# One hybrid mixer block with a conv-FFN on one core: where two of h's Strassen operands are split into high and low parts, when a gelu is issued, and the order of the last outputs

## The chip, the cores and the metric

The kernel runs on 1 core of one Trainium2 chip. The metric is the device time of one launch in microseconds (us). Engine names as the profile has them: PE (TensorE matmul), PEld (its weight loads), DVE (VectorE), ACT (ScalarE), POOL (GpSimd), SP (SyncE, here only a DMA queue). A second DMA queue is issued by POOL.

## The reference, cut to what matters

One transformer block on x of shape (1, 1024, 1024): token mixers, an output projection with residual and layer norm, and then the FFN, which is the part the change touches:

```python
def conv_ffn(h, w_up, conv_w, conv_b, w_down, grid_rows):
    a, g = jnp.split(h @ w_up, 2, axis=-1)                 # 1024 -> 2 x 2816
    a = dwconv3x3(a.reshape(...16 rows x 64 columns...), conv_w) + conv_b
    return (jax.nn.gelu(a, approximate=False) * g) @ w_down  # 2816 -> 1024

x_new = layer_norm(ALPHA * x_new + mx[5] * ffn_x, ln2_g[l], ln2_b[l])
```

Everything is float32. Products are made of two float32r parts of each operand, high and low: hi*hi + hi*lo + lo*hi, so three matmuls where one float32r matmul would be one.

## The kernel before

**Stages.** To about 690 us of the span: mixers, output projection, first layer norm and what prepares the FFN's first product. From there to about 1077 us `ffn_up`, then `ffn_down` to the end.

**ffn_up.** The 2816 hidden columns are 22 units f of 128 columns (hidden on partitions, 1024 tokens in the free dimension as two halves of 512). Each unit is made of seven block products in Winograd's form of Strassen's scheme; a product k is 12 matmuls of 128x128 by 128x512 (four pieces, three matmuls each). A unit's products run in the order 1, 2, 6, 5, 7, 3, 4 (`self.plan`, line 1111; units 1 and 2 are started by hand before the loop, lines 1213 to 1266, where the last two are product 4 of units 1 and 2; unit 0 is made without the scheme). Product 1, 6, 7, 4 add into one PSUM bank `u.x` (tag B), 2 into `u.zv[:, 0]`, 5 and 3 into `u.zv[:, 1]`, where `zv` is one of only two pairs of banks (tag A). `after(k)` (line 1333) is what follows a product:

- ACT copies banks out (`s`, `r`), DVE adds (`a`), ACT `centre` writes the middle tap of the 3x3 convolution into `zv`, DVE `conv` adds the other eight taps (8 instructions). So DVE does one unit's convolution while PE does the next unit's products.
- `b.prev.gelu()` comes after product 6 of the next unit (ACT reads the whole pair `zv`, which is then free), `finish` after its product 5 (DVE multiplies by the gate: `h` is ready, and its store to `hd[f]` is issued), `fetch` loads `hd[f - 11]` for the upper units.
- `b.made.sums()` (line 1410) comes after products 1 and 2 of the unit after that. For units 0 to 10 POOL makes h[:,0] - h[:,1] and SP stores it to `s3[f]`; for units 11 to 21 POOL makes two sums of h of units f and f - 11 and stores them to `s12[f - 11]`.

`prepare(n)` (line 1049) keeps the weights five products ahead: POOL makes the sums of raw weights (`combine`), ACT the high part (`wf[:, 0]`), and POOL the low part (`wf[:, 1]`, always one form later, `low`). All engines run their instructions in program order (`self.pinned`).

**From ffn_up to ffn_down.** In the last unit `down_first` (line 1287) makes the first three items of `ffn_down` ahead: high parts on ACT, low parts on POOL (tiles `dwh`, `dwl`, `dwv`). In `after(3)` of the last unit the sums of unit 20 stand ahead of its convolution (line 1364).

**ffn_down.** The same scheme over tokens, hidden and output columns: `plan` has 77 items (k, f), k in the order 1, 2, 6, 5, 3, 7, 4, f from 0 to 10; each item is 12 matmuls (4 blocks t of 128 tokens, three each). Products 1, 6, 7, 4 add into the banks `X[t]`, products 2, 5, 3 into `Y[t]`. For item i in iteration i: `load(i + 8)` (SP loads h's part and, where it is not on chip, w's part into a tile `raw`), `high(i + 5)` (ACT, two casts: h's half `[:, 0]` and w's half `[:, 1]` of the pair of tiles x = forms[i]), `low(i + 4)` (DVE, from item 5 on; two subtractions), then the matmuls. A pair of tiles is used again by item i + 8. For products 5, 7 (last 3 items) and 4 (last 5 items) the last items are held back and run together, block by block (`group`, line 1450): blocks 2 and 3 first, then 0, then 1.

**Outputs.** Tokens 0 to 511 (t 0 to 3) get their two column halves from X and Y during products 2 to 7, in pieces put into `todo`, of which one (two in the first five items of product 7) is issued at the end of an iteration. `out(t, c, bank, add)` (line 1561) returns the pieces: `begin` (DVE adds the bank to y), `mid` (POOL loads the residual x into a tile `fx`, DVE multiplies y by the gate), `end` (DVE: y = ALPHA x + y, then batch statistics). `chain` makes mean and 1/sigma of the rows (ACT does the square root), `last(t, c)` the layer norm's scale and shift, two DVE instructions on 512 columns, and the store. Tokens 512 to 1023 follow behind product 4: `out`, `chain`, `last` for blocks 2 and 3, then 0, then 1.

## Time and profile before

| | |
|---|---|
| time before, median of 3 runs | 1317.91 us (1316.45 to 1319.5) |
| the profiled execution's own time | 1315.14 us |
| its span, first to last instruction | 1313.4 us |
| PE busy | 1244.1 us, 95% |
| DVE busy | 1015.4 us, 77% |
| ACT busy | 550.9 us, 42% |
| POOL busy | 363.4 us, 28% |
| mean granted TensorE clock | 0.990 of full |
| HBM read, written | 168.32 MB, 39.08 MB |

"Busy" is the time in which an engine ran at least one instruction. PE at 95% does not say that it ran at its best rate; the granted clock tells which of two levels (1.2 and 2.4 GHz) it had. A share over the whole span says little for one stage, so the rows below are taken stage by stage. The time of a launch is a little longer than the span, since starting and ending stand around it.

### The profile page before, as it was taken

Reading aid. Unit: us, or ns where it says so; the run is one execution under the profiler, and the core shown is the slowest. Engines: PE = TensorE matmul, PEld = TensorE weight load, DVE = VectorE, ACT = ScalarE, POOL = GpSimd, SP = SyncE. Lnnn points to the kernel's source line nnn. Section 1 sums busy time; section 2 is a strip of 40 time slices with the busy share of each in tenths; the row PEclk is TensorE's granted clock in tenths of the full one; section 3 lists DMA queues with packets and bytes.
Section 4 is the critical chain, followed back from the end, with each engine's and each line's share of the span. In section 5 each row is a group of like instructions: output and inputs, shape, how many; then the busy total and the mean of one; then the engine's idle time right before and its main releaser. Section 6 shows DMA issues by size and latency. Waiting matters only on the chain. (4 is left out here: it accounts for less than half of the span.)

```text
span 1313.4 us, 17643 instructions
## 1 busy us (share of the span) xinstructions
PE 1244.1 (95%) x6348; PEld 1044.6 (80%) x6348; DVE 1015.4 (77%) x1790; ACT 550.9 (42%) x980; POOL 363.4 (28%) x309
## 2 busy tenths in 40 slices
PE   4999999999999989999998999999999999999993
PEld 3887888889888878777876788888888888888872
DVE  7968984686949768697797777777766776988797
ACT  4836444443332241345363444444344443545420
POOL 0000000000000000000017788888988872000020
PEclk9999999999999999999999999999999999999997
DMA  9763234104123054346564434542443268999242
GB/s 332 265 198 124 96 121 152 49 24 159 54 71 113 17 178 144 124 167 206 172 188 135 172 117 159 177 136 89 160 145 124 101 228 306 352 312 363 88 145 89
DMA packets 99672, 208.56 MB, mean 159 GB/s; under 512 B 10224, under 2 KB 31360, under 8 KB 99584
## 3 DMA queue, kind: packets, MB, share of 16 engines
q1 hardware_dynamic: 94784, 190.65, 42.7%
q0 software_dynamic: 4800, 16.78, 3.5%
q8 instruction: 50, 0.82, 0.2%
q14 instruction: 38, 0.31, 0.1%
HBM read 168.32 MB, written 39.08 MB: 158 GB/s over the span
## 5 line engine op out<-in xcount | busy, mean ns | idle before, releaser
L57 DVE SCALAR_TENSOR_TENSOR psA<-a,par,psA 128x945 f32<-128x945 f32 (+2 forms) x176 | 215.9, 1227 | 21.6 <-ACT psA L57 16.2
L57 PE MATMUL psA<-x,wf 128*128 128x512 f32 x708 | 172.2, 392 | 6.4 <-ACT h L57 3.4
L57 PE MATMUL psB<-xk,wf 128*128 128x512 f32 x672 | 176.7, 390 | 0.9 <-ACT s L57 0.9
L57 PEld LDWEIGHTS psA<-x,wf 128*128 128x128 f32 x708 | 133.8, 189 | 35.8 <-ACT psA L57 3.9
L57 PEld LDWEIGHTS psB<-xk,wf 128*128 128x128 f32 x672 | 126.1, 188 | 27.7 <-ACT s L57 1.3
L57 POOL DMA_DIRECT2D wd<-pk x16 | 8.7, 542 | 500.7 <-ACT pk L57 463.0
L57 PE MATMUL psA<-xh,wh 128*128 128x512 f32 x320 | 126.8, 396 | 2.0 <-ACT wh L57 1.2
L57 POOL TENSOR_TENSOR wf<-raw,wf 128x512 fp32r<-128x512 f32 x95 | 123.1, 1301 | 20.0 <-ACT wf L57 19.4
L57 PE MATMUL psA<-xh,wl 128*128 128x512 f32 x320 | 126.1, 394 | 0.1
L57 PE MATMUL psA<-xl,wh 128*128 128x512 f32 x320 | 125.9, 393 | 0.0
L57 PE MATMUL psB<-x,wf 128*128 128x512 f32 x384 | 104.7, 389 | 0.0
L57 PEld LDWEIGHTS psB<-x,wf 128*128 128x128 f32 x384 | 72.0, 188 | 15.3 <-issue 0.2
L57 ACT CAST wh<-r 128x512 fp32r<-128x512 f32 x76 | 44.5, 619 | 84.7 <-PE psA L57 57.3
L57 ACT CAST wf<-raw 128x512 fp32r<-128x512 f32 x95 | 58.7, 618 | 47.5 <-PE psA L57 27.4
L57 DVE TENSOR_TENSOR a<-psA,s 128x512 f32<-128x512 f32 x39 | 27.0, 691 | 60.6 <-PE psA L57 59.0
L57 PEld LDWEIGHTS psA<-xh,wh 128*128 128x128 f32 x320 | 60.2, 188 | 14.1 <-ACT wh L57 1.6
L57 PEld LDWEIGHTS psA<-xh,wl 128*128 128x128 f32 x320 | 60.2, 188 | 12.4 <-DVE wl L57 0.5
L57 PEld LDWEIGHTS psA<-xl,wh 128*128 128x128 f32 x320 | 60.2, 188 | 11.7 <-issue 0.2
L57 DVE TENSOR_TENSOR kq<-kq,F 128x1024 f32<-128x1024 f32 x56 | 67.5, 1216 | 0.2
L57 DVE TENSOR_TENSOR wl<-r,wh 128x512 fp32r<-128x512 f32 x76 | 49.9, 687 | 22.4 <-PE psB L57 13.2
L57 ACT CAST fh<-dr 128x512 fp32r<-128x512 f32 (+1 forms) x47 | 36.1, 768 | 72.8 <-DMA dr<-in_w_down 22.2
L57 PE MATMUL psB<-kq,A 128*128 128x128 f32 x448 | 60.4, 289 | 0.8 <-ACT A L57 0.7
(365 smaller groups left out, 2928.9 us busy)
## 6 DMA issues: line engine op xcount, KB each, us to landing
raw<-in_wup SPq DMA_DIRECT2D x38, 512.0 KB, 5.5
ada<-in_ada SPq DMA_DIRECT2D x32, 512.0 KB, 4.4
r<-in_win SPq DMA_DIRECT2D x56, 256.0 KB, 2.8
ex<-in_w_down SPq DMA_DIRECT2D x55, 256.0 KB, 5.4
dr<-hd SPq DMA_DIRECT2D x44, 256.0 KB, 5.4
hd<-h SPq DMA_DIRECT2D x20, 512.0 KB, 3.0
dr<-s SPq DMA_DIRECT2D x33, 256.0 KB, 5.3
adat<-in_ada SPq DMA_DIRECT2D x16, 512.0 KB, 7.0
```

The lines of the kernel that those rows point to most:

```text
L57: ins = f(*args, **kw)
```

## The change

Five edits.

1. `sums` now has three parts. For units 0 to 10 POOL's difference is written in place (into h[:,0]); for units 0 to 20 ACT also makes the high part of one operand (the difference for 0 to 10, h[:,1] for 11 to 20) into a new tile `hp`, POOL its low part, and both (512 KB) are stored: to `s3` for units 0 to 10, to the new `a22` for 11 to 20. They come after products 1, 2 and 6 of the unit after next.
2. In `ffn_down` the items of product 7 and those of product 4 but its last (`made(i)`, 21 items) no longer load h's part in `load(i)`. Instead `high(i)` issues two loads on SP of the ready high and low parts straight into the forms, and ACT and DVE each do one instruction of 512 columns (w's half) where they did two.
3. In the part by hand `u1.gelu()` moves from behind product 4 of unit 1 to ahead of `u2.centre(1)`, with one `prepare` ahead of it; the sums of units 0 and 1 move into unit 3.
4. The sums of unit 20 move from ahead of the last convolution to behind the last product of unit 21.
5. The second column half of tokens 0 to 511 is made in another order: `early` (gate and residual on what is in y) in product 3's first items, `late` (bank times gate into an `fx` tile) and `late2` (add, statistics) in product 7. `last` works on 1024 columns at once, but for the very last block (t = 1 of the second half), and product 7's `todo` shrinks from 17 pieces to 9.

```diff
-        u0.sums()[0]()
         u1.conv()
         go(u2, 3)
         tt(out=u2.a[:, 1], in0=u2.v, in1=u2.s[:, 1], op=ALU.add)
+        self.prepare(self.at + 5)
+        u1.gelu()
         u2.centre(1, u2.a[:, 1])
-        self.prepare(self.at + 5)
         go(u1, 4)
         self.prepare(self.at + 5)
-        u1.gelu()
         go(u2, 4)
         self.prepare(self.at + 5)
         u1.finish((u1.x, u1.r[1]))
         u2.conv()
-        u1.sums()[0]()
-        self.prev, self.made = u2, None
+        self.prev, self.made = u2, u0
...
+                if f == 3 and k in (7, 3, 4):
+                    u1.sums()[(7, 3, 4).index(k)]()
                 if f == last:
                     ahead(k)
+                    if k == 4:
+                        for part in self.made.sums():
+                            part()
...
-            if k in (1, 2) and b.made:
-                b.made.sums()[k - 1]()
+            if k in (1, 2, 6) and b.made:
+                b.made.sums()[(1, 2, 6).index(k)]()
...
-                if f == FT - 1:
-                    for part in b.made.sums():
-                        part()
                 self.conv()
...
             def one():
-                if f < FT // 2:
-                    s3 = b.S((2, 512), nm="s3")[:, 0]
-                    pool.tensor_tensor(out=s3, in0=self.h[:, 0], in1=self.h[:, 1], op=ALU.subtract)
-                    b.nc.sync.dma_start(b.s3[f], s3)
+                if lo:
+                    pool.tensor_tensor(out=src, in0=self.h[:, 0], in1=self.h[:, 1], op=ALU.subtract)
...
+                if not end:
+                    self.parts = b.S((2, 512), F32R, nm="hp")
+                    b.nc.scalar.copy(self.parts[:, 0], src)
+
+            def three():
+                if not end:
+                    p = self.parts
+                    pool.tensor_tensor(out=p[:, 1], in0=src, in1=p[:, 0].bitcast(F32), op=ALU.subtract)
+                    (b.nc.sync if f < FT - 2 else b.nc.gpsimd).dma_start((b.s3 if lo else b.a22)[f % (FT // 2)], p.bitcast(F32))
...
+            if made(i):
+                for j in range(2):
+                    nc.sync.dma_start(x[j][:, 0].bitcast(F32), (self.s3 if k == 7 else self.a22)[f][:, j])
+                nc.scalar.copy(x[0][:, 1], (t1 if k == 7 else t2)[f])
+                return
...
+            if made(i):
+                on.tensor_tensor(out=x[1][:, 1], in0=(t1 if k == 7 else t2)[f], in1=x[0][:, 1].bitcast(F32), op=ALU.subtract)
+                return
...
+            def early():
+                mid()
+                nc.vector.scalar_tensor_tensor(out=y, in0=x[0], scalar=ALPHA, in1=y, op0=ALU.mult, op1=ALU.add)
+
+            def late():
+                x[1] = dn.tile([P, 512], F32, tag="fx", bufs=3, name=self.name("fx"))
+                tt(out=x[1], in0=bank, in1=gate[:, half[c]], op=ALU.mult)
+
+            def late2():
+                tt(out=y, in0=y, in1=x[1], op=ALU.add)
+                nc.vector.bn_stats(out=st[t][:, c, :], in_=y)
...
-                            for c in range(2):
+                            for c in range(2) if t == 1 else (None,):
                                 last(4 + t, c)
...
-            if f == 0 and k in (6, 7):
-                o = [out(t, 0 if k == 6 else 1, Y[t], True) for t in range(4)]
+            if f == 0 and k == 6:
+                o = [out(t, 0, Y[t], True) for t in range(4)]
                 todo += [x[0] for x in o]
                 mids, ends = [x[1] for x in o], [x[2] for x in o]
-                if k == 7:
-                    fin = [lambda t=t, c=c: last(t, c) for t in range(4) for c in range(2)]
+            if f == 0 and k == 3:
+                o = [out(t, 1, Y[t], "early") for t in range(4)]
+                todo += [x[0] for x in o]
+            if f == 0 and k == 7:
+                if True:
+                    mids, ends = [x[1] for x in o], [x[2] for x in o]
+                    fin = [lambda t=t: last(t, None) for t in range(4)]
```

## Rows read from the trace of the kernel before

**Rows 1.** Busy time by stage: stretch, its length, busy us (and instructions) of PE, PEld, DVE, ACT and POOL, then granted TensorE clock, mean busy share of the DMA engines, GB/s.

```profile
690.00:735.00 45.00, 38.90 (x162) 31.01 (x162) 33.35 (x34) 18.53 (x30) 32.58 (x26) 0.96 0.40 136
735.00:1060.00 325.00, 325.00 (x1435) 268.93 (x1434) 237.70 (x239) 141.04 (x223) 276.87 (x214) 1.00 0.40 140
...
1108.00:1250.00 142.00, 142.00 (x626) 117.10 (x626) 123.73 (x189) 70.28 (x109) 3.82 (x7) 1.00 0.81 283
1250.00:1265.31 15.31, 12.46 (x50) 9.89 (x49) 15.13 (x24) 5.40 (x10) 2.70 (x5) 0.89 0.53 168
...
1285.90:1313.40 27.50, 6.77 (x30) 5.25 (x28) 22.43 (x47) 0.61 (x3) 0.55 (x1) 0.66 0.23 86
```

**Rows 2.** PE's waits from 690 us to the end (the one left out, 0.9 us, lies ahead of everything that the change touches): who <- whom, us in total, times, longest.

```profile
PE psA L57 <- ACT h L57: 3.4, 1, 3.4
PE psB L57 <- DVE fy L57: 2.9, 1, 2.9
PE psA L57 <- ACT psA L57: 1.8, 1, 1.8
...
PE psB L57 <- POOL dwl L57: 0.6, 1, 0.6
```

**Rows 3.** Timeline of the part by hand and of unit 3, 700 to 729 us, the rows of the chain only: start, length, engine, operation, tiles, [idle before <- what ended it]. The first `conv` is unit 1's, the second unit 2's; the first PE row is product 2 of unit 3, the second its product 3.

```profile
700.52 10.05 DVE L57 SCALAR_TENSOR_TENSOR psA<-a,par,psA 128x945 f32<-128x945 f32 x8
...
710.49 0.69 DVE L57 TENSOR_TENSOR a<-psB,s 128x512 f32<-128x512 f32 x1
711.27 0.78 ACT L57 ACTIVATE psA<-a,par 128x512 f32<-128x512 f32 x1 [6.89 <-DVE a L57]
...
713.01 1.01 ACT L57 ACTIVATE h<-psA 128x1024 f32<-128x1024 f32 x1
...
714.08 4.61 PE L57 MATMUL psA<-x,wf 128*128 128x512 f32 x12 [3.39 <-ACT h L57]
...
715.63 10.05 DVE L57 SCALAR_TENSOR_TENSOR psA<-a,par,psA 128x945 f32<-128x945 f32 x8
...
725.78 1.03 ACT L57 ACTIVATE h<-psA 128x1024 f32<-128x1024 f32 x1 [3.72 <-DVE psA L57]
...
727.83 0.78 ACT L57 ACTIVATE psA<-a,par 128x512 f32<-128x512 f32 x1
...
728.66 3.04 PE L57 MATMUL psA<-x,wf 128*128 128x512 f32 x12 [1.79 <-ACT psA L57]
```

**Rows 4.** Stretches just behind three waits of PE (columns as in rows 1): the clock is the third number from the end.

```profile
715.00:720.00 5.00, 5.00 (x17) 3.94 (x17) 4.89 (x5) 2.25 (x4) 5.00 (x5) 0.70 0.47 166
725.00:730.00 5.00, 3.21 (x15) 2.33 (x14) 4.24 (x5) 3.86 (x6) 2.03 (x2) 1.00 0.00 0
1260.00:1265.00 5.00, 3.94 (x11) 3.19 (x12) 4.93 (x9) 1.19 (x3) 0.54 (x1) 0.66 0.32 103
```

**Rows 5.** POOL inside the loop: one combine of unit 6's neighbourhood (807 us), one wait for ACT in an upper unit (1034 us), and the busy time of one upper unit's stretch (columns as in rows 1).

```profile
806.60 2.28 POOL L57 TENSOR_TENSOR raw<-raw,raw 128x512 f32<-128x512 f32 x1
1034.09 1.28 POOL L57 TENSOR_TENSOR wf<-s,wf 128x512 fp32r<-128x512 f32 x1 [1.78 <-ACT wf L57]
1017.50:1036.50 19.00, 19.00 (x86) 15.72 (x85) 13.08 (x13) 8.28 (x13) 16.39 (x14) 1.00 0.39 142
```

**Rows 6.** Timeline from ffn_up to ffn_down, 1078 to 1109 us: POOL's low part for item 1 and PE's wait for it; the store of the last unit's h; SP's load that waited for that store to land; DVE's wait for that load; PE's first matmuls of item 11.

```profile
1078.47 2.42 POOL L57 TENSOR_TENSOR dwl<-dr,dwh 128x1024 fp32r<-128x1024 f32 x1
1080.94 0.50 PE L57 MATMUL psB<-dwh,dwl 128*128 128x512 f32 x1 [0.57 <-POOL dwl L57]
1089.47 0.58 POOL L57 DMA_DIRECT2D hd<-ex  x1 [3.61 <-ACT fh L57]
1098.11 1.11 SPq L57 DMA_DIRECT2D ex<-in_w_down  x2
1105.28 0.69 DVE L57 TENSOR_TENSOR tk<-ex,tk 128x512 f32<-128x512 f32 x1 [5.73 <-DMA ex<-in_w_down]
...
1108.27 0.47 PE L57 MATMUL psB<-fh,fl 128*128 128x512 f32 x1
```

**Rows 7.** Timeline around the end of product 3 and of product 7 in ffn_down: DVE's first reads of Y behind product 3; DVE's reads of X[0] and X[1] behind product 7; PE's first matmul of product 4 and its first of the next item. The last row is a group of DVE's low parts from 1226 to 1258 us (count, busy us, mean ns).

```profile
1226.29 1.37 DVE L57 TENSOR_TENSOR fy<-fy,psB 128x512 f32<-128x512 f32 x2 [4.13 <-PE psB L57]
1260.23 1.28 DVE L57 TENSOR_TENSOR fy<-fy,psB 128x512 f32<-128x512 f32 x2
1261.06 0.77 PE L57 MATMUL psB<-dw 128*128 128x512 f32 x1 [2.85 <-DVE fy L57]
1265.31 0.39 PE L57 MATMUL psB<-fh 128*128 128x512 f32 x1
L57 DVE TENSOR_TENSOR fl<-dr,fh 128x512 fp32r<-128x512 f32 x7 | 4.8, 685 | 0.0
```

**Rows 8.** The tail: the first instruction of `chain` for blocks 2 and 3, DVE's first layer-norm instruction of these blocks (eight of them follow one another), the instruction that comes next, the first output instruction of block 0, and, from the first layer norm of the kernel, the same operation on 1024 columns (min/median/max ns, first and last start). The last row is the loads of h's sums in ffn_down (count, KB, median us from issue to landing).

```profile
1290.01 0.33 DVE L57 BATCH_NORM_AGGREGATE finmv<-bnd 128x2 f32<-128x12 f32 x2
...
1291.48 0.75 DVE L57 SCALAR_TENSOR_TENSOR fy<-fy,finmv,ln_g 128x512 f32<-128x512 f32 x1
1297.28 0.69 DVE L57 TENSOR_TENSOR fy<-psB,gate 128x512 f32<-128x512 f32 x1
...
L57 DVE SCALAR_TENSOR_TENSOR ly<-ly,mvt,ln_g x8: 1272/1276/1282, 564.2 to 643.2; 128x1024 f32<-128x1024 f32 x8
...
dr<-s SPq DMA_DIRECT2D x33, 256.0 KB, 5.3
```

More of the change, by code (lines that the diff above doesn't have):

```diff
@@ L244, in build @@
             self.s12 = [self.dp.tile([P, 2, 512], F32, name=f"s12_{f}") for f in range(FT // 2)]
-            self.s3 = [self.dp.tile([P, 512], F32, name=f"s3_{f}") for f in range(FT // 2)]
+            self.s3, self.a22 = ([self.dp.tile([P, 2, 512], F32, name=f"{n}_{f}") for f in range(FT // 2)] for n in ("s3", "a22"))
             self.xr = [self.dp.tile([P, 2, 512], F32, name=f"xr{j}") for j in range(4)]
@@ L1412, in sums @@
             b, pool, f = self.b, self.b.nc.gpsimd, self.f
+            lo, up, end = f < FT // 2, f >= FT // 2, f == FT - 1
+            src = self.h[:, 0] if lo else self.h[:, 1]
             def one():
-                if f < FT // 2:
-                    s3 = b.S((2, 512), nm="s3")[:, 0]
-                    pool.tensor_tensor(out=s3, in0=self.h[:, 0], in1=self.h[:, 1], op=ALU.subtract)
-                    b.nc.sync.dma_start(b.s3[f], s3)
+                if lo:
+                    pool.tensor_tensor(out=src, in0=self.h[:, 0], in1=self.h[:, 1], op=ALU.subtract)
                 else:
@@ L1423, in two @@
             def two():
-                if f >= FT // 2:
+                if up:
                     s = self.s12
@@ L1427, in two @@
                     (b.nc.sync if f < FT - 2 else b.nc.gpsimd).dma_start(b.s12[f - FT // 2], s)
-            return one, two
+                if not end:
[6 more added lines that the diff above has]
+                    (b.nc.sync if f < FT - 2 else b.nc.gpsimd).dma_start((b.s3 if lo else b.a22)[f % (FT // 2)], p.bitcast(F32))
+            return one, two, three
     HF = FT // 2
@@ L1467, in raw, with made @@
             return dn.tile([P, 2, 512], F32, tag="raw", bufs=6, name=self.name("dr"))
+        def made(i):
+            k, f = plan[i]
+            return k == 7 or k == 4 and f < HF - 1
         def load(i):
@@ L1474, in load @@
                 return
+            if made(i):
+                return
             r = raws[i] = raw()
             h = {1: (0, 0), 2: (0, 1), 3: (0, 1), 4: (1, 1)}.get(k)
-            src = self.h_part(*h, f) if h else self.s3[f][:, :] if k == 7 else self.s12[f][:, 1 if k == 6 else 0]
+            src = self.h_part(*h, f) if h else self.s12[f][:, 1 if k == 6 else 0]
             nc.sync.dma_start(r[:, 0], src)
@@ L1534, in low @@
             on = nc.gpsimd if i < 5 else nc.vector
+            if made(i):
+                on.tensor_tensor(out=x[1][:, 1], in0=(t1 if k == 7 else t2)[f], in1=x[0][:, 1].bitcast(F32), op=ALU.subtract)
+                return
             if k in (2, 3):
@@ L1581, in end @@
                 self.residual(x[0], y, st[t][:, c, :])
+            def early():
[7 more added lines that the diff above has]
+                nc.vector.bn_stats(out=st[t][:, c, :], in_=y)
+            if add == "early":
+                return early, late, late2
             if add:
@@ L1602, in last @@
             m, r = stat[t]
-            y, s = ys[t][:, half[c]], half[c]
+            s = slice(0, D) if c is None else half[c]
+            y = ys[t][:, s]
             nc.vector.scalar_tensor_tensor(out=y, in0=y, scalar=m, in1=lng[:, s], op0=ALU.subtract, op1=ALU.mult)
```

## The prediction

> **What bounds the kernel now.** I read the busy time by stage first, then PE's waits, then the timeline around each wait. The stages say where anything can be won. From 735 to 1060 us and from 1108 to 1250 us PE is busy for the whole stretch at the full clock [rows 1], so an edit that only unloads another engine there wins nothing. What is left lies in three places: 690 to 735 us (PE busy 38.90 of 45 us, clock 0.96), 1250 to 1265.31 us (12.46 of 15.31, clock 0.89), and the tail behind 1285.9 us, which DVE fills (22.43 of 27.50 us). PE's waits name them: 3.4 us for a gelu, 1.8 us for a `centre`, 2.9 us for DVE's read of `fy` and 0.6 us for POOL's `dwl` [rows 2].
>
> The clock belongs to these places. Behind the waits of 3.39 and 2.85 us the granted clock was 0.70 and 0.66 over the next 5 us, and a product took 4.61 us; behind the wait of 1.79 us it was 1.00, and a product took 3.04 us [rows 3, 4]. So a wait of about 3 us costs some 1.6 us more than itself.
>
> **Edit 3, the earlier gelu.** Unit 1's convolution ends at 700.52 + 10.05 = 710.57. ACT then did unit 2's `centre` (711.27), two casts, and the gelu only at 713.01; PE got the banks at 714.08 [rows 3]. Now the casts can run before 710, and the gelu comes first: start 710.65, end 711.7, PE at 711.75, a wait of 1.06 us with the clock up. That is 2.3 us of wait and 1.7 us of slow clock (in steady running matmuls start 325 / 1435 = 0.2265 us apart [rows 1] and last 0.39, so a product of 12 fills 2.72 us and lasts 2.88, not 4.61) that go.
>
> But that isn't the gain, for DVE is late next. Unit 2's convolution needs its `centre` (711.7 + 0.78 = 712.5) and, on DVE, two gate products ahead of it (two such take 1.28 us [rows 7]): it begins at 712.95 instead of 715.63 and ends at 723.0. From there the chain to product 3 of unit 3 is unchanged: gelu, a cast, a copy, `centre` on ACT, from 725.68 to 728.66 before, 2.98 us [rows 3]; so product 3 begins at 726.0. PE could begin it at 711.75 + 4 x 2.72 = 722.6. A wait of 3.2 us stands there in place of 1.79, and I expect the clock to fall behind it, for 1.7 us. Gain: 728.66 - 726.0 = 2.7, less 1.7, which is 1.0; I take 1.2, since the wait is a little shorter than 3.39. Bounds: 2.9 if the clock stays up; -1 if POOL, with the sums of two units in unit 3 (15 operations of 276.87 / 214 = 1.29 us [rows 1], 19.4 us where a unit has 7 x 2.72 = 19.04), comes up to 2 us late for a form.
>
> **Edit 1, the parts of h.** Per unit POOL gets one operation more of 1.29 us, ACT a cast of 0.6 us (141.04 us for 223 instructions [rows 1]), and SP 256 KB (units 0 to 10) or 512 KB more to store. Cost taken: nothing. POOL is busy 16.39 of 19.0 us in an upper unit, and waits 1.78 us for ACT at one point of it [rows 5], and `three` stands ahead of that wait and fills it: 0.5 us are left. ACT's cast falls into an idle stretch after product 2. The DMA engines are at 0.40 [rows 1]. If the cover went, each unit would be longer by what POOL lacks (below). A store on SP now waits for `three`, and behind it in SP's queue stand the fetch of h and the raw weights, both needed a unit or more later.
>
> One row speaks against: a combine beside DVE's reduction of `ada` took 2.28 us instead of 1.28 [rows 5]. The Trainium skill states such a rule (GPSIMD Engine Reference, 1. Specifications: the SBUF interfaces are shared with VectorE, with contention where a VectorE instruction has two SBUF inputs). By that rule each new operation could take 1 us more. It would use up the 0.5 us that are left and raise the chance of the rival on POOL. `three` falls beside the convolution, whose second input is in PSUM, so I add nothing.
>
> **Edit 4, unit 20's sums.** Two sums (2 x 1.29) and a store (0.58) go from ahead of the low part of item 1, so POOL makes it at 1075.3 instead of 1078.47, and the wait of 0.57 us at 1080.94 goes. What is late next: POOL stores the last unit's h at 1089.47, SP's load waits for it to land (1098.11), DVE for that load (1105.28), and item 11's second matmul was already late by 0.08 us at 1108.27, for it came 0.31 us behind the first, not 0.23 [rows 6]. That chain starts at the last convolution, which does not move against ffn_up. So PE arrives earlier and waits there: gain 0. Bounds: +0.1, and -1.9 if the extra store of 512 KB delays the landing of that h (at the 283 GB/s of the next stage [rows 1]). POOL itself should be free at 1075.3 + 2.42 + 3 x 1.29 + 2 x 0.58 + 4 x 1.29 = 1087.9, 1.6 us before the store.
>
> **Edit 2, ready-made halves.** It takes 11 DVE instructions out of product 7, 10 out of product 4, and as many ACT casts; it adds 21 loads of 256 KB, net, on SP. A form is free when item i - 8 is done, its loads are issued then, and it is needed 7 items later, 19 us; loads of this size land in 5.3 us [rows 8]. For items 71 to 73 the buffers come free only with the held group, at 1258, and the first is needed five items later, 1271.9: still 13 us. Cost 0; bounds 0 to 2 us, should a landing take three times as long. Nothing but the last item's load and the final stores is queued behind them on SP. The gain is DVE's time, counted with edit 5.
>
> **Edit 5, the seam and the tail.** PE went idle at 1258.21, where by its pace the next matmul could have begun at 1258.05; but DVE read X[0] and X[1] only at 1260.23, and PE began product 4 at 1261.06 and its next item at 1265.31 instead of 1258.05 + 2.72 = 1260.77: 4.54 us lost [rows 7]. DVE was simply behind. Behind Y (ready at 1226.3) it now has, up to item 65's low part: 12 output instructions and 6 low parts of 0.69 (12.4 us), `chain` with 1.5 to 1.6, and 8 layer-norm instructions of 1.28 on 1024 columns (10.2 us) [rows 7, 8]: 24.2 us, so free at 1250.5, or a good microsecond sooner, since neighbours overlap by 0.1 (two in 1.28). PE's held group, 36 matmuls, begins at 1258.05 - 8.15 = 1249.9 and takes the low part of item 65 some 1.5 us later: just covered. X[1] is then read as PE finishes it: 1258.21 + 0.05 + 0.69 = 1258.95 against 1258.05 + 3 x 0.2265 = 1258.73, so 0.25 us of wait remains. Gain 4.54 - 0.25 = 4.3. Bounds: 0 (DVE still late) to 4.5. `early` puts 4 x 1.3 us into product 3; DVE is free for 18.3 us of the 142 from 1108 to 1250 [rows 1], and the residual's loads are issued long before.
>
> In the tail DVE has no pause, so each microsecond counts. Eight instructions of 512 columns took 1297.28 - 1291.48 = 5.80 us, so a pair 1.45. A pair on 1024 columns takes 1.45 + 2 x (1.276 - 0.75) = 2.50: 5.0 in place of 5.8, and 2.5 in place of 2.9 for block 0 [rows 8]. Gain 1.15, bounds 0.6 to 1.3 (stores of 512 KB may land later).
>
> **Sum.** 1.2 + 0 + 0 + 4.3 + 1.15 = 6.65 us. The profiled execution, 1315.14 us with a span of 1313.4, becomes 1308.5 with 1306.75. The median of the runs is 2.77 above the profiled execution, so the predicted time is 1317.91 - 6.65 = 1311.3, by itself 1309.5 to 1313.3 (the runs of before spread over 3 us, and the terms by about as much).
>
> **The rivals.**
> - *The clock stays up* behind the 3.2 us at 726 us: 1.7 more, 1309.6. For it: the wait is shorter than the 3.39 us that brought 0.70. Against: 2.85 us brought 0.66 [rows 4]. The Trainium skill says of that clock that the same kernel can get a different number of slow matmuls from run to run (TensorE: Matmul & The Clock Gate, What's actually happening); by that this rival could be true of some runs only, and no run here shows it.
> - *The seam stays.* DVE's new order still ends late in product 7, and PE waits 2.9 us and loses its clock again: gain 1.2 + 1.15, 1315.6. For it: only 1 to 2 us of slack in my count. Against: 9 pieces in place of 17.
> - *POOL sets the pace, slower.* In the ten upper units POOL has 14 operations x 1.29 = 18.1 us. If its wait for ACT of 1.78 us stayed beside the new operation, a unit would take 19.9 us in place of 19.04, 8.6 us in ten units: 1317.9 - 6.65 + 8.6 = 1319.9. It decides from the point where POOL's lag behind PE passes the five products of `prepare`. For it: 16.39 of 19.0 us and the stretched 2.28 [rows 5]. Against: the wait stands behind the new operation and absorbs it.
> - *The last h comes late.* POOL's extra work in edit 4 delays the chain of rows 6 by 1.5 to 4 us: 1314.
> - *The loads are late.* SP issues them in order behind buffers that PE frees; if issue and landing took 22 us in place of 5.3, items would follow each other by 22 / 7 = 3.14 us, 0.42 more in each of 21: 1320. For it: SP's queue is in order. Against: 19 us to spare.
>
> **How the numbers follow.** Forecast 0.56, clock up 0.18, seam 0.08, POOL's pace 0.06, late h 0.10, late loads 0.02. A measurement tells 0.2% (2.6 us) from no change, so faster means under 1315.3: the forecast, the clock, and most of late h, 0.82. The seam and the rest of late h are within, 0.10; POOL's pace and late loads are slower, 0.08. The range, 1307.0 to 1316.0, reaches from the second case and the upper bounds of edits 3 and 5 to the seam.
>
> **What would show it.** PE's 3.39 us at 714 becomes about 1.1, and a wait of about 3.2 us for ACT's `centre` stands near 723 to 726 with a clock near 0.7 behind it; no wait for `dwl` near 1080, but one of under 1 us near item 11; PE's 2.85 us at 1261 becomes under 0.5 with the clock at 1.00; 735 to 1060 stays fully busy with POOL near 17.7 of 19 us; from the end of blocks 2 and 3 to the end of the span 26.3 us in place of 27.5. A PE idle inside the loop, or a wait for loads in products 7 or 4, would make the prediction wrong.

## The result, and the profile after

The kernel after took 1308.02 us (median of 4 runs, 1307.47 to 1308.87) where the kernel before, beside it, took 1318.7 us (1316.45 to 1320.82): a ratio of 0.992, 95% interval 0.9901 to 0.9938. Two more sets of runs gave ratios of 0.9932 (0.9915 to 0.9949) and 0.9948 (0.9931 to 0.9964). The gain was 10.7, 9.4 and 7.6 us by medians; forecast were 6.65 us, 1311.3 us as a time, 1307.0 to 1316.0 as a range.

The profiled execution took 1308.36 us with a span of 1306.6. The two profiles must not be subtracted as they are. The stage that the change doesn't touch ran longer this time: unit 1's convolution began at 702.96 us, before at 700.52 [rows 3]. Counted from there, the end came 603.6 us later, against 612.9: 9.3 us gained.

Busy time by stage of the kernel after (stretch, its length, busy us and instructions of PE, PEld, DVE, ACT, POOL, granted clock, DMA share, GB/s):

```profile
690.00:735.00 45.00, 39.97 (x174) 32.14 (x173) 35.55 (x36) 18.98 (x31) 32.44 (x26) 1.00 0.39 129
735.00:1060.00 325.00, 325.00 (x1436) 268.94 (x1435) 239.06 (x239) 150.41 (x240) 299.86 (x233) 1.00 0.46 166
...
1108.00:1250.00 142.00, 142.00 (x627) 117.25 (x626) 125.03 (x185) 61.61 (x93) 6.51 (x12) 1.00 0.88 310
1250.00:1265.31 15.31, 15.21 (x68) 12.27 (x67) 10.94 (x19) 3.12 (x5) 1.09 (x2) 1.00 0.92 303
```

Against [rows 1], the loop is as full as it was, with POOL busy 23 us longer in it. In the stretch around the seam (1250 to 1265.31 us) PE has gone from 12.46 to 15.21 us at the full clock, and DVE from 15.13 to 10.94; the kernel after is 1.3 us further on in its work where that stretch begins. PE's waits from 690 us to the end are down to three (who, for whom, us in total, times, longest), the last of them ahead of the change:

```profile
PE psA L57 <- ACT psA L57: 3.1, 1, 3.1
PE psA L57 <- ACT h L57: 1.1, 1, 1.1
PE psB L57 <- ACT s L57: 0.9, 1, 0.9
```

Timeline of the part by hand, rows of the chain (as [rows 3]):

```profile
702.96 10.05 DVE L57 SCALAR_TENSOR_TENSOR psA<-a,par,psA 128x945 f32<-128x945 f32 x8
713.11 1.02 ACT L57 ACTIVATE h<-psA 128x1024 f32<-128x1024 f32 x1 [5.77 <-DVE psA L57]
714.19 3.01 PE L57 MATMUL psA<-x,wf 128*128 128x512 f32 x12 [1.06 <-ACT h L57]
715.38 10.06 DVE L57 SCALAR_TENSOR_TENSOR psA<-a,par,psA 128x945 f32<-128x945 f32 x8
725.53 1.02 ACT L57 ACTIVATE h<-psA 128x1024 f32<-128x1024 f32 x1 [4.98 <-DVE psA L57]
726.45 0.61 ACT L57 CAST wf<-raw 128x512 fp32r<-128x512 f32 x1
726.96 0.59 ACT L57 COPY r<-psA 128x512 f32<-128x512 f32 x1
727.58 0.78 ACT L57 ACTIVATE psA<-a,par 128x512 f32<-128x512 f32 x1
728.41 3.02 PE L57 MATMUL psA<-x,wf 128*128 128x512 f32 x12 [3.05 <-ACT psA L57]
```

Here product 3 takes 3.02 us behind its wait of 3.05: no fall of the clock in this execution. From the convolution to product 3 it is 25.45 us, before 28.14. The seam: DVE's low parts of items 64 and 65 (half of each), its reads of X[0] and X[1], PE's matmul that waits for the second, PE's next item. And the tail: the first layer-norm instruction of blocks 2 and 3, the instruction behind the four, the same two for block 0, and the last layer-norm instruction of all:

```profile
1246.98 1.29 DVE L57 TENSOR_TENSOR dw<-tv,dw 128x512 fp32r<-128x512 f32 x2
...
1254.91 0.69 DVE L57 TENSOR_TENSOR fy<-fy,psB 128x512 f32<-128x512 f32 x1 [0.76 <-PE psB L57]
1256.95 0.69 DVE L57 TENSOR_TENSOR fy<-fy,psB 128x512 f32<-128x512 f32 x1 [1.35 <-PE psB L57]
1257.69 0.50 PE L57 MATMUL psB<-dw 128*128 128x512 f32 x1
1259.87 0.39 PE L57 MATMUL psB<-fh 128*128 128x512 f32 x1
...
1286.05 1.28 DVE L57 SCALAR_TENSOR_TENSOR fy<-fy,finmv,ln_g 128x1024 f32<-128x1024 f32 x1
1291.08 0.68 DVE L57 TENSOR_TENSOR fy<-psB,gate 128x512 f32<-128x512 f32 x1
1294.58 1.28 DVE L57 SCALAR_TENSOR_TENSOR fy<-fy,finmv,ln_g 128x1024 f32<-128x1024 f32 x1
1297.10 0.68 DVE L57 TENSOR_TENSOR fy<-psB,gate 128x512 f32<-128x512 f32 x1
...
1302.83 0.75 DVE L57 SCALAR_TENSOR_TENSOR fy<-fy,finrs,ln_b 128x512 f32<-128x512 f32 x1
```

DVE now waits for PE at both reads; PE loses 0.26 us there (1257.69 where its pace gives 1257.43). Four instructions take 5.03 us where eight took 5.80 [rows 8].

To say where time goes, the span from unit 1's convolution on is cut at three points that every trace has: PE's first matmul of ffn_down (item 0), its first matmul of item 3 (the first on a tile `fh`), its last matmul.

| us | convolution to item 0 | item 0 to item 3 | item 3 to last matmul | last matmul to end |
|---|---|---|---|---|
| before | 376.75 | 9.02 | 206.38 | 20.72 |
| after | 373.96 | 8.16 | 202.15 | 19.34 |
| gained | 2.79 (edit 3) | 0.86 (edit 4) | 4.23 (seam) | 1.38 (tail) |

The experiments ask three things: is the first column's 2.79 us a property of the kernel, which of the edits 2 and 5 closed the seam, and how near POOL is to its limit.

### The profile page after: what moved, and what is told of

The parts are those of the page before. It is cut to its first block, busy times and chain, and to the rows that moved or that the text cites. A ratio compares the mean times of both kernels' runs of the same rounds, so it can differ in the third digit from the quotient of the medians.

```text
span 1306.6 us, 17721 instructions
## 1 busy us (share of the span) xinstructions
PE 1243.9 (95%) x6348; PEld 1045.8 (80%) x6348; DVE 1005.1 (77%) x1759; ACT 551.0 (42%) x980; POOL 386.8 (30%) x327
## 5 line engine op out<-in xcount | busy, mean ns | idle before, releaser
L57 PEld LDWEIGHTS psB<-kq,A 128*128 128x128 f32 x448 | 55.9, 192 | 5.9 <-ACT A L57 5.5
```

Source lines behind the costliest of these rows:

```text
L57: ins = f(*args, **kw)
```

## The experiments

### Edit 3 and the clock: the gelu put back, twice, and the kernel after, twice more

```diff
-        self.prepare(self.at + 5)
-        u1.gelu()
         u2.centre(1, u2.a[:, 1])
+        self.prepare(self.at + 5)
         go(u1, 4)
         self.prepare(self.at + 5)
+        u1.gelu()
         go(u2, 4)
```

> The kernel after, with the gelu of unit 1 put back behind product 4 of unit 1 (edit 3 undone, but for where the sums of units 0 and 1 stand). Theory 1 (the early gelu is worth what the two traces show from unit 1's convolution to unit 3's product 3, 28.14 - 25.45 = 2.69 us): the wait at unit 3's product 2 is again near 3.4 us with a granted clock near 0.70 behind it, the wait at product 3 falls to about 1.8, and the time is 2.3 to 3.1 us above the kernel after. Theory 2 (it is worth the 1.2 us of the forecast, the rest of the difference being chance of one profiled execution): 0.8 to 1.6 us above. Either way the rest of the trace stays as it is after the change.

Measured: 1308.79 us, ratio 0.996 (0.9947 to 0.9973). The wait of 3.39 us is back, with a clock of 0.50 over the 5 us behind it (near 0.70 was expected), and the one at product 3 is 0.61 us (1.8 was expected). Convolution to item 0: 376.79 us, before 376.75. So against the first profile of the kernel after it loses 2.83 us there, as theory 1 has it. The two kernels were not run side by side here, so their times are not set against each other.

But the old outputs (below), which share edit 3, had another clock at that place. Hence the kernel after again, without any edit:

> The kernel after once more, beside its relatives on one chip. In its first profile the wait at unit 3's product 3 was 3.05 us with the clock at 1.00 behind it; with the old order of the outputs, which changes nothing there, it was 3.05 us with the clock at 0.66. Theory 1 (at waits of about 3 us the fall of the clock is chance): from product 3 to the first item of ffn_down it takes 348.5 or 350.2 us, by chance, and the runs spread by those 1.7 us. Theory 2 (something else in the other kernel brought the fall): 348.5 again, clock 1.00. Time 8.5 to 10 us below before in the same call, if the forecast's terms as measured (2.7 + 0.9 + 4.3 + 1.3) hold on this chip too.

Measured: 1304.62 us, ratio 0.9932 (0.9915 to 0.9949). The wait was 3.05 us again, and this is the stretch behind it (length, PE busy, clock, DMA share, GB/s):

```profile
723.03:728.03 5.00, 5.00 (x12) 0.50 0.28 108
```

The clock was on its lower level for the whole stretch: 12 matmuls in 5 us instead of 22. Convolution to item 0 took 376.82 us, as long as before the change: in this execution edit 3 gave nothing. Theory 1 holds, with a larger stake than it named (2.9 us, not 1.7).

> The kernel after a third time, as the measure for the two beside it. From unit 1's convolution to the first item of ffn_down it took 373.96 us in the first profile (clock 1.00 behind the wait at unit 3's product 3) and 376.82 in the second (0.50). If the fall is chance, this profile shows 374 to 377 with the clock to match.

Measured: 1306.49 us, ratio 0.9948 (0.9931 to 0.9964), 374.00 us:

```profile
723.71:728.71 5.00, 5.00 (x22) 1.00 0.28 108
```

> The kernel after with the gelu of unit 1 put back, a second time, now beside the kernel after. Its first profile took 376.79 us from unit 1's convolution to the first item of ffn_down, the kernel before 376.75. Theory 1 (edit 3 is worth its shorter waits, 2.7 us, less what the clock takes back behind product 3, which is 1.7 to 2.9 us in most executions): the median is 0 to 1.2 us above the kernel after. Theory 2 (the clock mostly stays up, as in the first profile): 2 to 3 us above.

Measured, beside the third: 1307.88 us, ratio 0.9962 (0.9946 to 0.9977), convolution to item 0 376.68 us. It is 1.4 us above the kernel after by the medians, a little more than theory 1 allows and less than theory 2, and the two intervals overlap. All traces together say it better:

| kernel | wait at product 3 | clock, 5 us behind it | convolution to item 0 |
|---|---|---|---|
| gelu late: before, put back twice, outputs alone, unit 20 alone | 0.61 to 2.05 | 1.00 in all | 376.62 to 376.79 |
| after, first and third | 3.05 | 1.00 | 373.96, 374.00 |
| after, again | 3.05 | 0.50 | 376.82 |
| old outputs; one more POOL operation | 3.05 | 0.66 | 375.66, 375.61 |
| copy first | 2.92 | 0.50 | 377.03 |
| longer wait | 4.29 | 0.66 | 376.91 |
| centre behind | 0.72 | 1.00 | 371.76 |

The first row holds a finding of its own: with the gelu late the clock falls every time behind the 3.39 us at product 2 (0.50 to 0.70), yet the total doesn't move by 0.2 us, for a wait stands behind it that a slower PE only shortens (2.05 to 0.61 us). With the gelu early, the last wait stands at product 3, nothing behind it absorbs the fall, and the total depends on chance. The five executions in rows two to four gain 2.79, 2.75, -0.07, 1.09 and 1.14 us against before: 1.5 on the mean. Four of them have the same code up to item 0; the fifth has one more POOL operation in each upper unit, long behind product 3, and no wait of PE from there to item 0.

### A longer wait at product 3

```diff
-                nc.scalar.copy(self.r[0], self.zv[:, 1])
+                for _ in range(3 if f == 3 else 1):
+                    nc.scalar.copy(self.r[0], self.zv[:, 1])
```

> The kernel after, with the copy that frees the bank for unit 3's product 3 made three times over (same result), so the wait there becomes 3.05 + 1.1 = 4.1 to 4.2 us. Theory 1 (the longer the wait, the surer the fall: 3.39 us brought it in all four traces that have it, 2.8 to 3.1 in two of four): the clock falls to 0.5 to 0.7 behind it, from product 3 to ffn_down's first item it takes 350.2 us or more, and the time is 1.1 + 1.7 = 2.8 us above a run of the kernel after whose clock stays up. Theory 2 (the length doesn't matter here): clock 1.00, 1.1 us above.

Measured: 1308.29 us, ratio 0.9958 (0.9945 to 0.9972); wait 4.29 us.

```profile
726.67:731.67 5.00, 5.00 (x15) 0.66 0.28 108
```

Convolution to item 0 took 376.91 us, 2.9 above a run of the kernel after whose clock stays up: theory 1's sum. Its reason is only half borne out. From 690 us on the clock fell behind every wait of 3.39 us and more (seven, with one of 3.98 us in the run with two more POOL operations below), but behind two shorter ones it was lower over the next 5 us (0.50) than behind this one. The length of one wait doesn't tell how far it falls.

### What product 3 waits for: the copy first

```diff
             elif k == 6:
-                if b.prev:
+                if b.prev and f != 3:
                     b.prev.gelu()
...
                 nc.scalar.copy(self.r[0], self.zv[:, 1])
+                if f == 3:
+                    b.prev.gelu()
                 self.centre(0, self.a[:, 0])
             elif k == 7:
                 tt(out=self.r[1], in0=self.x, in1=self.r[0], op=ALU.add)
+                if f == 3:
+                    b.prev.finish()
...
```

> The kernel after, with the gelu of unit 2 moved on ACT from ahead of to behind the copy that frees the bank for unit 3's product 3, and its gate products on DVE behind unit 3's addition of product 7. Theory 1 (product 3 waits only because ACT takes its instructions in order, the copy standing behind a gelu that waits for the convolution): the wait of 3.05 us falls under 0.3 us, nothing takes its place, and the time is 2.7 to 3.1 us below the kernel after. Theory 2 (DVE is the bound there: the convolution ends at 725.4 us, and its addition after product 7 frees the bank of product 4): PE waits 1.2 to 1.6 us at product 4 instead, and 1.4 to 1.8 us are gained. Theory 3 (the pair of banks comes free too late for unit 4): the wait stands at unit 4's product 2, nothing gained.

Measured: 1306.3 us, ratio 0.994 (0.9925 to 0.9955). Nothing of the wait went, and none of the three theories held. Timeline:

```profile
722.24 0.58 ACT L57 COPY r<-psA 128x512 f32<-128x512 f32 x1 [4.98 <-DVE a L57]
722.72 1.03 ACT L57 ACTIVATE h<-psA 128x1024 f32<-128x1024 f32 x1
723.63 0.79 ACT L57 ACTIVATE psA<-a,par 128x512 f32<-128x512 f32 x1
724.48 2.07 PE L57 MATMUL psA<-x,wf 128*128 128x512 f32 x4 [2.92 <-ACT psA L57]
```

The copy ends at 722.82 us, and product 3 still waits until `centre` ends (724.42). That instruction writes `zv[:, 0]`, product 3 adds to `zv[:, 1]`: they share no data, only the pair of banks, which is one tile. And the copy itself waited for DVE's `a`, which was issued ahead of it.

### Centre behind product 3

```diff
...
+                if f == 3:
...
+                    nc.scalar.copy(self.r[0], self.zv[:, 1])
+                    tt(out=self.a[:, 0], in0=self.zv[:, 0], in1=self.s[:, 0], op=ALU.add)
+                    b.prev.gelu()
+                    return
...
                 tt(out=self.a[:, 1], in0=self.zv[:, 1], in1=self.s[:, 1], op=ALU.add)
+                if f == 3:
+                    self.centre(0, self.a[:, 0])
                 self.centre(1, self.a[:, 1])
```

> The kernel after, with unit 3's copy that frees the bank first of all, unit 2's gelu behind it, and the centre of unit 3's first half (which writes the other bank of the pair) issued behind product 3 instead of ahead of it. With the copy alone moved, product 3 still began right when that centre ended (724.42 and 724.48 us), so the centre is what it waits for. Theory 1 (that is so, and only through the pair of banks being held as one tile): the wait of 2.9 to 3.05 us falls to at most 0.7 us (DVE's addition, which reads the pair behind unit 2's convolution), the clock stays at 1.00 behind it, and from unit 1's convolution to ffn_down's first item it takes 371.3 to 372; 2 to 2.7 us less than the kernel after where its clock stays up, 4 to 5.5 where it falls. Theory 2 (the next in the chain takes its place: the addition after product 7, or unit 4's first centre, now one instruction later): a wait of 1 to 2 us at product 4 or in unit 4, and under 1.5 us gained.

Measured: 1303.62 us, ratio 0.9924 (0.9909 to 0.9938); the kernel after, beside it, took 1306.49. Timeline:

```profile
720.18 0.59 ACT L57 COPY r<-psA 128x512 f32<-128x512 f32 x1 [1.61 <-PE psA L57]
722.84 0.68 DVE L57 TENSOR_TENSOR a<-psA,s 128x512 f32<-128x512 f32 x1
723.58 3.01 PE L57 MATMUL psA<-x,wf 128*128 128x512 f32 x12 [0.72 <-DVE a L57]
```

PE's waits from 690 us to the end:

```profile
PE psA L57 <- ACT h L57: 1.1, 1, 1.1
PE psB L57 <- ACT s L57: 0.9, 1, 0.9
PE psA L57 <- DVE a L57: 0.7, 1, 0.7
```

Theory 1 holds to the tenth: 0.72 us of wait for DVE's addition (which reads the other bank of the pair, the same tie), clock 1.00, 371.76 us, no new wait. This kernel beats both: 10.5 us below before and 2.9 below after by medians of runs made side by side (the intervals of the two ratios overlap from 0.9931 to 0.9938, so the 2.9 rests as much on the traces: 2.2 us to the kernel after with its clock up, 5.1 with it down).

### The seam: the outputs as before, and the outputs alone

First the kernel after without edit 5:

```diff
...
-            if f == 0 and k == 6:
+            if f == 0 and k in (6, 7):
-                o = [out(t, 0, Y[t], True) for t in range(4)]
+                o = [out(t, 0 if k == 6 else 1, Y[t], True) for t in range(4)]
...
-                            for c in range(2) if t == 1 else (None,):
+                            for c in range(2):
...
```

> The kernel after, with edit 5 undone: the outputs in the order of before and the layer norm in pieces of 512 columns, while DVE still has half of each low part in products 7 and 4. Theory 1 (the new order closes the seam, as the forecast has it): without it DVE is late again, PE waits 2 to 2.9 us for X at the seam, its clock falls, and the time is 1.2 + 4.3 = 5.5 us above the kernel after. Theory 2 (DVE's time is what counts, wherever it comes from): ten low parts halved behind Y give 10 x 0.60 = 6.0 us, more than the 2.0 us by which DVE was late, so the seam's wait stays near 0.25 us and only the tail is longer, by 1.2 us.

Measured: 1308.63 us, ratio 0.9955 (0.9942 to 0.9968). DVE's reads of X:

```profile
1259.20 1.28 DVE L57 TENSOR_TENSOR fy<-fy,psA 128x512 f32<-128x512 f32 x2 [0.92 <-PE psA L57]
1261.24 0.69 DVE L57 TENSOR_TENSOR fy<-fy,psB 128x512 f32<-128x512 f32 x1 [0.76 <-PE psB L57]
1263.28 0.69 DVE L57 TENSOR_TENSOR fy<-fy,psB 128x512 f32<-128x512 f32 x1 [1.35 <-PE psB L57]
```

DVE idles 0.92 us ahead of the first read: in time, with the old order. From the last read to the last matmul it takes 30.28 us, in the kernel after too. From the last matmul to the end it takes 20.79 us instead of 19.34, the tail. Theory 2: the halves alone close the seam. (It also took 0.62 us more from item 3 to the last matmul, most of it at item 11, where its only wait, of 0.27 us, puts the second matmul 0.65 us behind the first, and its clock fell behind product 3. The kernel after was not run beside it.)

Then the reverse, the kernel before with edit 5 alone:

```diff
...
+            if f == 0 and k == 3:
+                o = [out(t, 1, Y[t], "early") for t in range(4)]
+                todo += [x[0] for x in o]
...
+                            for c in range(2) if t == 1 else (None,):
```

> The kernel before with edit 5 alone: new order of the outputs and the layer norm on 1024 columns, but both halves of h split in ffn_down as before. Theory 1 (the new order alone closes the seam): a wait of 0.25 us there, gain 4.3 + 1.2 = 5.5 us against before. Theory 2 (the halves were needed too): the kernel after has DVE idle for 2.20 us ahead of its first read of X and takes 6.0 us less of low parts behind Y; with these 6.0 us back DVE reads X[0] and X[1] some 2.5 us later than it does after the change, PE waits 1.2 to 2 us at the seam, and the gain is 2 to 4 us.

Measured: 1311.65 us, ratio 0.9976 (0.9965 to 0.9987), 3.1 us below before. PE's second matmul of a held item, the first on the next banks, and DVE's last read of X:

```profile
1252.35 1.10 PE L57 MATMUL psA<-dw,dw 128*128 128x512 f32 x2 [0.47 <-DVE dw L57]
1256.59 0.39 PE L57 MATMUL psB<-fh 128*128 128x512 f32 x1
1260.87 0.69 DVE L57 TENSOR_TENSOR fy<-fy,psB 128x512 f32<-128x512 f32 x1 [0.16 <-PE psB L57]
```

The long wait is gone here too, with the clock at 1.00, but PE lost time earlier: from the first matmul of the second of the three held items on block 2 (1251.49) to their first on block 0 it took 5.10 us, 3.40 in the kernel after, for it picks up each low part as DVE makes it. Item 3 to last matmul 204.51 us: 1.9 gained, and 1.0 in the tail. Theory 2 has the size right (2 to 4 us) but not the place: with the order alone DVE reads X in time, and PE loses 1.7 us at the low parts of the held items instead. The halves alone close the seam wholly.

### Edit 4 alone

```diff
-                if f == FT - 1:
-                    for part in b.made.sums():
-                        part()
                 self.conv()
```

(with the same loop over the parts put behind product 4 of the last unit)

> The kernel before with edit 4 alone: unit 20's sums behind the last product of unit 21. Theory 1 (the forecast: the gain is lost again at item 11, where PE waits for DVE's load of the last unit's h): no wait for dwl near 1080 us, a wait of 0.5 to 0.9 us at item 11, the time unchanged within 0.2 us. Theory 2 (in the kernel after PE kept the time because the last h lands sooner, and that comes from this edit): no wait at either place, gain 0.6 to 0.9 us. Theory 3 (the last h lands sooner by another edit): as theory 1, with the load of h issued by SP 8.6 us behind its store, not 7.6.

Measured: 1314.78 us, ratio 0.9999 (0.9991 to 1.0007). Its waits at the seam and at item 11:

```profile
PE psB L57 <- DVE fy L57: 2.8, 1, 2.8
...
PE psB L57 <- DVE fl L57: 0.4, 1, 0.4
```

The stretch behind the first of them (columns as for product 3):

```profile
1260.29:1265.29 5.00, 5.00 (x22) 1.00 0.34 113
```

Item 0 to item 3 is 8.16 us, as in the kernel after; at item 11 the second matmul is 0.74 us behind the first where 0.23 is its pace, so 0.51 of the 0.86 is lost again and 0.35 stays. Theory 1, and 3 as far as the landing goes. The store of the last unit's h took 8.5 us to land here and in the kernel before, 8.8 with the outputs alone. With edits 1 and 2 it took 7.3 to 7.8 in all profiles that show no wait at item 11, and 8.2 in the one that shows 0.27 us (the old outputs). What lands it sooner wasn't tried. The second finding is the seam: a wait of 2.83 us and no fall of the clock. From PE's first matmul behind it to its last it took 30.20 us, before 31.61: 1.4 us of the 4.23 in the table is this chance.

### POOL's reserve

```diff
-                    pool.tensor_tensor(out=p[:, 1], in0=src, in1=p[:, 0].bitcast(F32), op=ALU.subtract)
+                    for _ in range(3 if up else 1):
+                        pool.tensor_tensor(out=p[:, 1], in0=src, in1=p[:, 0].bitcast(F32), op=ALU.subtract)
```

> The kernel after, with the subtraction that makes the low part of h made three times over for units 11 to 20 (the same result each time), so two more POOL operations of 1.25 us in each of ten units. It tests the rival in which POOL sets the pace. In the kernel after POOL waits 1.33 us for ACT once in an upper unit. Theory 1 (that is all its slack): each unit then needs 16 x 1.25 = 20.0 us of POOL where PE takes 19.04, a lag of 1.0 us a unit that the five products of lead (13.6 us) absorb until the end; 735 to 1060 us stays fully busy, and POOL comes some 8 to 10 us late to the low parts of ffn_down's first items: 4 to 9 us slower than the kernel after. Theory 2 (the lead is less than five products in fact): PE waits in the loop already, and 10 us or more are lost. Theory 3 (POOL has more slack than the wait shows): within 1 us of the kernel after.

Measured: 1322.42 us, ratio 1.0073 (1.0053 to 1.0093), 17.8 us above the kernel after beside it. PE's two costliest waits (the first with the 1.0 us that lies ahead of the change):

```profile
PE psB L57 <- ACT s L57: 8.1, 7, 1.3
PE psB L57 <- POOL fl L57: 4.7, 2, 4.0
```

How one of the six that lie behind the change comes about, in the timeline: ACT's cast behind a POOL sum, ACT's copy behind the cast, PE behind the copy.

```profile
985.13 0.62 ACT L57 CAST wf<-raw 128x512 fp32r<-128x512 f32 x1 [1.87 <-POOL raw L57]
985.66 0.58 ACT L57 COPY s<-psB 128x512 f32<-128x512 f32 x1
986.29 0.50 PE L57 MATMUL psB<-xk,wf 128*128 128x512 f32 x1 [1.32 <-ACT s L57]
```

Theory 2: the first of these waits stands at 965.6 us, and from there on they follow each other 20.6 us apart, where PE's pace gives 19.04 a unit: 1.6 us lost in each. The lead is not five products, since ACT's queue is in order: a cast that waits for POOL holds up the copy that frees PE's next bank.

> The kernel after, with the subtraction that makes the low part of h made twice for units 11 to 20 (same result), so one more POOL operation of 1.25 us a unit, where two more cost PE 1.3 us in each unit from the sixteenth on. Theory 1 (POOL's wait for ACT of 1.33 us a unit is its slack): 15 x 1.25 = 18.75 us of 19.04, no wait of PE in the loop, and from 735 to 1060 us PE is busy all the time; at the items of ffn_down nothing changes beyond 0.5 us. Theory 2 (part of that wait is bound to stay, since ACT's cast comes no sooner): POOL lags by 0.5 to 1 us a unit, and PE waits in the last units or at item 11, 2 us or more in all.

Measured, in a single run: 1311.21 us. The loop stays full (325.00 of 325), but at the fourth item of ffn_down PE waits for POOL and its clock falls. Timeline:

```profile
1085.38 0.50 PE L57 MATMUL psB<-fh,fl 128*128 128x512 f32 x1 [1.07 <-POOL fl L57]
...
1086.60 0.50 PE L57 MATMUL psB<-fl,fh 128*128 128x512 f32 x1 [0.72 <-POOL fl L57]
```

The stretch from there:

```profile
1085.38:1090.38 5.00, 4.28 (x12) 0.74 1.01 339
```

From item 3 to the last matmul it took 206.14 us, 4.0 more than after. Theory 2: in the upper units POOL runs without a pause, one unit from 1021.78 to 1041.17 us, 19.39 where PE takes 19.04. One operation more gives 20.64, the pace at which PE's waits came with two more. So the kernel after has 1.25 - 0.35 = 0.9 us of POOL to spare in a unit, less than one operation.

## Why the prediction was right, and where not

**The whole.** 6.65 us forecast; 10.7, 9.4 and 7.6 measured by medians of three sets of runs, 9.2 on the mean. The terms below give 1.5 + 0.9 + 4.2 + 1.4 = 8.0 us. The measured time lay inside the range, 3.3 us below the number. Of that the terms explain 1.4 us on the mean (8.0 - 6.65) and 2.6 in the first profile (9.26 - 6.65): edit 4, and the chance of the clock. What is left is no larger than the scatter of the stage ahead of the change, which moved unit 1's convolution from 697.6 to 707.0 us in these profiles; that it comes from there is not shown.

**Edit 3 (forecast 1.2, bounds -1 to 2.9; measured 1.5 on the mean, -0.07 to 2.79).** The chain came out as worked out: a wait of 1.06 us at product 2, the gelu the bound, 3.05 at product 3 (3.2 was said), product 3 earlier by 2.69 (2.7). The clock was the open step. The first profile made the rival "the clock stays up" look true; the further profiles show that both happen, at a price of 0, 1.7 or 2.9 us. The error was to treat it as two worlds, of which one is the case: it came out differently from one execution to the next. The kernel after had a clock of 1.00, 0.50 and 1.00 behind the same 3.05 us, and three kernels whose code is the same up to there had 0.66. The Trainium skill says, of a kernel's start, that the same kernel can get a different number of slow matmuls from run to run (TensorE: Matmul & The Clock Gate, What's actually happening); these traces show the same behind a wait in the middle of a kernel.

**What product 3 waits for.** The prediction took the chain of four ACT instructions as given ("unchanged"). Of the four the copy hands on data and the centre holds the other bank of the same tile; the gelu and the cast only stand in ACT's queue. The real tie is the pair of banks. Read so, the chain offers 2.2 to 5 us more, which the kernel with the centre behind took.

**Edit 1 (0; right).** PE is busy 325.00 of 325 us, and POOL's 23 us more came out of its waiting. The groups of POOL's rows in that stretch, after (count, busy, mean ns, idle ahead):

```profile
L57 POOL TENSOR_TENSOR wf<-s,wf 128x512 fp32r<-128x512 f32 x34 | 44.0, 1294 | 23.8 <-ACT wf L57 23.8
...
L57 POOL TENSOR_TENSOR hp<-h,hp 128x512 fp32r<-128x512 f32 x18 | 23.5, 1308 | 0.0
```

The new operation takes 1308 ns, and all of them fall beside the convolution, whose second input is in PSUM. The Trainium skill names contention for VectorE instructions with two SBUF inputs (GPSIMD Engine Reference, 1. Specifications); the trace agrees in that none shows here. The reserve that the prediction named, 0.5 us a unit, is 0.9. Its rival on POOL was right in kind but had the wrong deciding point: not a lag of five products, but the first low parts of ffn_down (one operation more) or ACT's queue (two more).

**Edit 4 (forecast 0, bounds +0.1 to -1.9; measured 0.86 in the kernel after, 0.35 alone).** Here a step failed: "PE arrives earlier and waits there". Alone it does, for 0.5 us; in the kernel after the last h landed in 7.5 us instead of 8.5, and PE never met it. The prediction took the landing time from one row of before as fixed; what shortened it stays open, since edits 1 and 2 were not run apart. (The 0.31 us that the prediction read at item 11 of before stand between its second matmul and its third, not its first and second; the 0.08 us are the same.) POOL was free when forecast (1087.73 us, 1087.9 was said).

**Edits 2 and 5 (4.3 at the seam; measured 4.2).** The low part of item 65 ended at 1248.27 us, 0.3 us ahead of PE's held group (1248.59); the forecast had it 0.6 us behind the group's start, "or a good microsecond sooner". The wait left is 0.26 us (0.25). But the prediction counted the DVE time of both edits in one sum, under edit 5, and did not say which of the two closes the seam. The runs show that edit 2's halves (6.0 us of DVE time by estimate, ten low parts at 0.6 us) do it alone, while the order alone leaves 1.7 us. And 1.4 us of the gain is the clock, which may or may not fall in the kernel before.

**The tail (1.15; measured 1.38).** 5.03 and 2.52 us stand where 5.0 and 2.5 were forecast; the 0.23 us on top lie behind DVE's last instruction, where the end of the span came 2.99 us after it instead of 3.21.

## What to carry to other kernels

Follow a clock's fall to the next wait on the same engine: where one stood behind it the fall was free in these traces, where none did it cost 0 to 2.9 us by chance, and a single profile shows one draw. Before an instruction order is taken as a chain of needs, ask of each link whether it hands on data or only a tile, for a pair of banks held as one tile ties two halves that have nothing to do with each other. And when two edits relieve the same engine, run each without the other: the sum may be right while the credit is wrong.

## What the runs showed that was not expected

The length of a wait doesn't decide the clock alone: 2.83 us left it at 1.00 and 2.85 brought it to 0.70 at the same seam, 3.05 gave 1.00, 0.66 and 0.50 at the same product, and 4.29 gave 0.66. At product 3 waits up to 2.05 us never moved it, nor did the 1.3 us that came every 20.6 us in the run with two more POOL operations. Elsewhere shorter ones did: 1.07 and 0.72 us close together at the start of ffn_down brought 0.74, and in the kernel after, far ahead of the change, a single wait of 1.94 us at 484.28 us brought 0.66:

```profile
484.30:489.30 5.00, 5.00 (x28) 0.66 0.58 171
```

And a reserve of less than one POOL operation a unit didn't show as a wait inside the loop at all when it was overdrawn by 0.35 us a unit: it showed 4 us of loss at the stage behind it.
